# A hybrid decoder layer: other root, store and tile slots in its last product

## The chip, the core and the metric

The kernel runs on one core of a Trainium2 chip. The metric is the time of one execution on the device, in microseconds (us). TensorE is called PE, VectorE DVE, ScalarE ACT, GpSimd POOL and SyncE SP, as in the profile.

## What is computed

One decoder layer over 1024 tokens (plus 16 meta tokens) of width 1024, in float32. The part that matters here is the end of it:

```python
def rmsnorm(x, g):
    y = x * rsqrt(mean(x * x, axis=-1, keepdims=True) + EPS)     # EPS = 1e-6
    return y * g
...
    h = h + rmsnorm(mix, g_post_mix)
    u = rmsnorm(h, g_pre_ffn)
    f = square(relu(u @ w_ff1)) @ w_ff2      # w_ff1: 1024 x 4096, w_ff2: 4096 x 1024
    h = h + rmsnorm(f, g_post_ffn)
    return h[:, N_META:]
```

Before it come an input projection, sliding-window attention with sinks, a gated linear recurrence, and an output projection whose result is normed and added to the residual stream. The kernel writes that sum to `out` and later adds the normed result of the second feed-forward product to it.

## The kernel before

**Precision.** A float32 operand is split into a rounded part and a rest: `split` (L93 to L98) rounds on ACT (L95) and subtracts on DVE (L98). Each product is three matmuls, `mm3` (L121 to L125): high by high, high by low, low by high.

**The two feed-forward products.** Both are cut into 2 x 2 blocks and done with seven products of blocks instead of eight. For the second, `PLAN` (L1029 on) lists seven entries, i = 0 to 6: which blocks of the activations are added or subtracted, which blocks of `w_ff2` are, and into which parts of the result the product goes and with which sign. The sum runs over 512 rows of a block in eight steps, q = 0 to 7, so there are 56 steps n in order (i, q). In each, four token tiles j = 0 to 3 of 128 rows get six matmuls of 512 columns each. In i = 6 the last tile's 512 columns are done as two halves of 256 in two PSUM banks (`col_parts`).

**A step's operands.** `fetch_2(n)` (L1046) loads the one or two blocks of weights that the step needs, 512 KB each, on SP's queue. Where two blocks are added, some steps load the second with an accumulating DMA from POOL's queue into the first one's tile (L1055): for i < 6 those with q % 3 < 2, for i = 6 those whose second tag in `LASTW` is None. The others load both, and `prep_2(n)` (L1062) adds or subtracts them on DVE, splits the weights, combines and splits the activations. The loop fetches four steps ahead, from n = 45 on six.

**Slots.** All tiles in SBUF come from tagged pools (`bufs`, L55): "raw" has 2 slots, "e" 2, "ws" 4, "a" 16, "b" 17, "c" 8, "d" 4. A tile waits for a free slot of its tag. During the second product "a" holds the activation blocks fb["12"] and fb["21"] (eight each), the lower token tiles' sums facc["0", j], the broadcast gain and the finished tiles. "b" holds part of fb["11"], the upper tiles' sums facc["1", j], the combined and split activations, and four raw weight tiles of i = 6.

**Order.** A scheduler orders each engine's instructions by program order among those that are ready on its own clock of estimated durations, and gives out the slots as it goes. `behind` (L105) and `lut` (L81) add edges without a wait: an instruction comes behind a named one in its engine's order; `lut` chains all activations that use a table function (exponential, sigmoid, tanh, square root, GeLU) in program order.

**Norms of the result.** The result has eight token tiles: the upper four, facc["1", j], are complete after i = 5, the lower four, facc["0", j], only after i = 6.
- `rstd_of` (L155) turns partial means of squares into 1 / sqrt(sum + EPS): one add with EPS on DVE (L160; on POOL where there is one part), then a power of -0.5 on POOL (L164).
- `finish_early(j)` (L1120), for tiles 4 to 7, runs inside i = 5 and at the start of i = 6: two squares with their sums on ACT (L1117), `rstd_of`, one scaling on DVE (L1124), and an accumulating store to `out` from POOL's queue (L1128).
- `finish_half(j)` (L1132) runs in steps q = 1 to 4 of i = 6, for tiles 0 to 3: the square of the right half, which is complete by then (L1137). For tiles 2 and 3 it loads the rows of `out` into a "d" tile, adds EPS on POOL (L1144) and multiplies the right half by the gain on DVE (L1145).
- `finish_late(j)` (L1148) ends a tile. The last three steps (`LAST`) are done tile by tile, so that tile 0 ends first and tile 3 last. Tiles 0 and 1: add the product (L1154), square on ACT, `rstd_of`, one scaling (L1158) and an accumulating store from POOL (L1162). Tiles 2 and 3: add the product, squares and their sum on DVE (L1165), power on POOL (L1173), times the gain (L1175), then for each half scale and add the loaded rows (L1177) and a plain store, from SP and from ACT (L1180).

Of the kernel before, what the change touches and what calls it, by code (L numbers as in the profile page):

```python
# [9 lines left out]
F32 = mybir.dt.float32  # L10
F32R = mybir.dt.float32r
AF = mybir.ActivationFunctionType
ALU = mybir.AluOpType
# [3 lines left out]
P = 128  # L17
# [10 lines left out]
EPS = 1e-6  # L28
# [9 lines left out]
def hybrid_layer(  # L38
# [6 lines left out]
    nc = tc.nc  # L45
# [3 lines left out]
    const = ctx.enter_context(tc.tile_pool(name="const", bufs=1))  # L49
    small = ctx.enter_context(tc.tile_pool(name="small", bufs=4))  # L50
# [7 lines left out]
    def slot(tag, shape, dt=F32):  # L58
        uid[0] += 1
        return slab.tile(shape, dt, tag=tag, name=f"{tag}{uid[0]}", bufs=bufs[tag])  # L60
# [20 lines left out]
    def lut(*args, **kwargs):  # L81
        ins = nc.scalar.activation(*args, **kwargs).ins
        if last_lut[0] is not None:
            tc.add_manual_dep(
                ins, last_lut[0],
                mybir.DependencyInfo(
                    mybir.DependencyClass.NoSync, mybir.DependencyReason.DATA
                ),
                reason="lut",
            )  # L90
        last_lut[0] = ins.name
# [13 lines left out]
    def behind(name, *inss):  # L105
        for ins in inss:
            tc.add_manual_dep(
                ins, name,
                mybir.DependencyInfo(
                    mybir.DependencyClass.NoSync, mybir.DependencyReason.DATA  # L110
                ),
                reason="order",
            )
# [38 lines left out]
    half_pow = const.tile([P, 1], F32, name="half_pow")  # L152
    nc.gpsimd.memset(half_pow, -0.5)

    def rstd_of(ssq_parts, n=P):  # L155
        ms = small.tile([P, 1], F32, name="ms", tag="ms")
        if len(ssq_parts) == 1:
            nc.gpsimd.tensor_scalar(ms[:n], ssq_parts[0], EPS, None, op0=ALU.add)
        else:
            nc.vector.scalar_tensor_tensor(  # L160
                ms[:n], ssq_parts[0], EPS, ssq_parts[1], op0=ALU.add, op1=ALU.add
            )
        rs = small.tile([P, 1], F32, name="rs", tag="rs")
        nc.gpsimd.tensor_tensor(rs[:n], ms[:n], half_pow[:n], op=ALU.pow)  # L164
        return rs[:n]


# [249 lines left out]
    for b in range(2):  # L417
        pv = bank("pt", (P, 4, P))
        for i in range(4):
            o = NMETA + (4 * b + i) * P  # L420
# [366 lines left out]
    def combine(dst, x0, x1, op):  # L787
        return nc.vector.tensor_tensor(dst, x0, x1, op=op).ins  # L788
# [48 lines left out]
    def early(b, p0, hl):  # L837
        raw = slot("raw", [P, 2, 4, P])
        for k in range(2):
            w1_load(raw[:, k], b, p0 + k, 0, 1)  # L840
        split(*hl, raw)
        return {p0 + k: (hl[0][:, k], hl[1][:, k]) for k in range(2)}
# [49 lines left out]
    def p1(p, w):  # L892
        ya[p] = bank(("acc", "s")[p // 2 % 2])
        product(ya[p], w, b11, True)
        nc.scalar.copy(block("11", p), ya[p])
# [6 lines left out]
    for t in range(8):  # L902
# [12 lines left out]
        if t == 6:  # L915
            b21 = operand(u2f[0][2:4])
            hl = slot("b", ESH, F32R), slot("e", ESH, F32R)
            a11_early.update(early(0, 2, hl))

    for p in range(2):  # L920
        p1(p, a11_early[p])
    for p in range(2):
# [93 lines left out]
    def product_by_parts(acc, w, op):  # L1016
# [22 lines left out]


    LASTW = [
        ("raw", None), ("e", "raw"), ("b", None), ("b", None), ("raw", "e"), ("b", None),
        ("e", "raw"), ("b", None),
    ]

    def fetch_2(n):  # L1046
        i, q = steps[n]
        wx = PLAN[i][1]
        tags = (("raw", "e"), ("e", "raw"))[n % 2] if i < 6 else LASTW[q]
        raws = []  # L1050
        for (a, b), tag in zip(wx[:2], tags):
            if len(wx) == 3 and wx[2] is ADD and raws and (
                q % 3 < 2 if i < 6 else tag is None
            ):
                nc.gpsimd.dma_start(raws[0], w2v[q, a, b], accum_op=ADD)  # L1055
                break
            r = slot(tag, [P, 2, 512])
            nc.sync.dma_start(r, w2v[q, a, b])
            raws.append(r)
        return raws  # L1060
# [24 lines left out]
    w_low = [None]  # L1085
# [27 lines left out]
    COLS = (slice(0, 512), slice(512, 1024))  # L1113

    def squares(sq, src, n):
        p_ = small.tile([P, 1], F32, name=f"sq{n}", tag=f"sq{n}")
        nc.scalar.activation(sq, src, AF.Square, scale=RMS_SC, accum_out=p_)  # L1117
        return p_

    def finish_early(j):  # L1120
        acc = facc["1", j]
        o = slot("a", [P, D])
        ssq = [squares(o[:, c], acc[:, c], n) for n, c in enumerate(COLS)]
        nc.vector.scalar_tensor_tensor(  # L1124
            o, acc, rstd_of(ssq), gffn_b, op0=ALU.mult, op1=ALU.mult
        )
        t = 4 + j
        nc.gpsimd.dma_start(out[t * P : (t + 1) * P, :], o, accum_op=ALU.add)  # L1128
# [3 lines left out]
    def finish_half(j):  # L1132

        o = slot("a", [P, D])
        acc, c = facc["0", j], COLS[1]
        ssq = small.tile([P, 1], F32, name=f"late{j}", tag=f"late{j}", bufs=1)
        nc.scalar.activation(  # L1137
            o[:, c], acc[:, c], AF.Square, scale=RMS_SC, accum_out=ssq
        )
        h = None  # L1140
        if j > 1:
            h = slot("d", [P, D])
            nc.sync.dma_start(h, out[j * P : (j + 1) * P, :])
            nc.gpsimd.tensor_scalar(ssq, ssq, EPS, None, op0=ALU.add)  # L1144
            behind(w_low[0], combine(o[:, c], acc[:, c], gffn_b[:, c], ALU.mult))  # L1145
        halves[j] = h, o, ssq

    def finish_late(j, y, parts):  # L1148

        h, o, ssq = halves[j]  # L1150
        acc = facc["0", j]
        for k, c in enumerate(parts):
            yield k
            ins = combine(acc[:, c], y[k], acc[:, c], ALU.add)  # L1154
            if k == 1:
                behind(w_low[0], ins)
            if j < 2:
                w_low[0] = nc.vector.scalar_tensor_tensor(  # L1158
                    o, acc, rstd_of([squares(o[:, c], acc[:, c], 0), ssq]), gffn_b,
                    op0=ALU.mult, op1=ALU.mult,  # L1160
                ).ins.name
                nc.gpsimd.dma_start(out[j * P : (j + 1) * P, :], o, accum_op=ALU.add)  # L1162
                continue
            part = small.tile([P, 1], F32, name=f"part{k}", tag=f"part{k}")
            nc.vector.tensor_tensor_reduce(  # L1165
                out=o[:, c], in0=acc[:, c], in1=acc[:, c], scale=RMS_SC * RMS_SC,
                scalar=ssq, op0=ALU.mult, op1=ALU.add, accum_out=part,
            )
            ssq = part
        if j < 2:  # L1170
            return
        rs = small.tile([P, 1], F32, name="rs", tag="rs")
        nc.gpsimd.tensor_tensor(rs, ssq, half_pow, op=ALU.pow)  # L1173
        c = COLS[0]
        combine(o[:, c], acc[:, c], gffn_b[:, c], ALU.mult)  # L1175
        for c, eng in zip(COLS[::-1], (nc.sync, nc.scalar)):
            w_low[0] = nc.vector.scalar_tensor_tensor(  # L1177
                o[:, c], o[:, c], rs, h[:, c], op0=ALU.mult, op1=ALU.add
            ).ins.name
            eng.dma_start(out[j * P : (j + 1) * P, c], o[:, c])  # L1180
# [37 lines left out]
    for n, (i, q) in enumerate(steps):  # L1218
        while fetched < min(n + (4 if n < 45 else 6), len(steps)):
            raw_2[fetched] = fetch_2(fetched)  # L1220
            fetched += 1
        if n + 1 < len(steps):
            late = w_low[0]
            ready[n + 1] = prep_2(n + 1, "a" if n + 1 >= len(steps) - LAST else "ws")
        if q == 0:
            old = None if i == 0 else accs
            accs = [[bank(("acc", "s", "pt", "o")[j])] for j in range(4)]
            if i == 6:

                evict(5, 0, old[0][0], late)  # L1230
                accs[3] = [accs[3][0][:, :256], bank("acc")[:, :256]]
        if n < len(steps) - LAST:
            for j in range(4):
                for acc, cols in zip(accs[j], col_parts(i, j)):
                    step_mm(acc, j, q, ready[n], cols)
            del ready[n]
        if old and (q > 0 or i < 6) and q < 4:
            evict(i - 1, q, old[q][0], late)
        if i == 5 and q == 0:
            gffn_b = slot("a", [P, D])  # L1240
            nc.scalar.dma_start(gffn_b, g_post_ffn[0].partition_broadcast(P))
        if (i, q) in EARLY:
            finish_early(EARLY.index((i, q)))
        if i == 6 and 1 <= q < 5:
            finish_half(q - 1)
# [36 lines left out]
```

## Time and profile before

| | us |
|---|---|
| median of 3 runs | 974.02 (973.7 to 976.03) |
| the profiled execution | 972.95 |
| its span, from the first to the last instruction | 971.1 |
| PE busy in it | 953.7 |
| last product (i = 6), PE | about 918 to 964 |

The profile shows one execution. A row of an engine says when it starts, how long it takes, the engine, the line, the operation, the tiles written and read, the shapes, and in brackets how long the engine idled before and what released it. Starts are microseconds from the start of the span. Matmuls are pipelined, so one's row overlaps the next one's; the distance of their starts tells the rate. A DMA's row on an engine is its issue; the time to landing is told by the DMA view. The granted clock of PE was 0.999 in the mean.

### The profile page before, as it was taken

The page shows a single profiled execution, that of the slowest core. Times are in us where ns is not written, and L with a number is a line of the kernel's source. Part 1 is how long each engine was busy: PE and PEld are TensorE (multiplying, and loading weights), DVE is VectorE, ACT ScalarE, POOL GpSimd, SP SyncE. Part 2 cuts the span into 40 slices and gives each one's busy share as a digit, 9 for nine tenths or more (in the row PEclk, how much of TensorE's full clock was granted, in tenths as well). Part 3 has the DMA queues.
Part 4 walks back from the last instruction along what each step waited for, and adds up shares of the span by engine and source line. Part 5 has one row for each costly group of instructions (what it writes and reads, how often), then busy time and mean ns, then how long its engine had stood idle before and what let it go on. Part 6 is the DMA issues. An engine that isn't in the chain of part 4 may idle for free.

```text
span 971.1 us, 12490 instructions
## 1 busy us (share of the span) xinstructions
PE 953.7 (98%) x4782; PEld 803.0 (83%) x4782; DVE 674.6 (69%) x997; ACT 502.0 (52%) x809; POOL 82.4 (8%) x109
## 2 busy tenths in 40 slices
PE   6999999999999999999999999999999999999997
PEld 6999999888878887888888878888888888888786
DVE  6679997775976686665645465468557676779694
ACT  6646673567844554343555556555433344445350
POOL 4100000000002100000000000000111000003152
PEclk9999999999999999999999999999999999999999
DMA  9002001012234466576522264323678765548923
GB/s 296 23 1 66 23 23 44 23 48 64 84 119 144 159 207 209 173 251 209 198 87 87 97 206 125 114 87 114 172 176 198 186 224 187 184 163 195 223 80 87
DMA packets 88219, 130.13 MB, mean 134 GB/s; under 512 B 13624, under 2 KB 52552, under 8 KB 88160
## 3 DMA queue, kind: packets, MB, share of 16 engines
q1 hardware_dynamic: 79792, 107.33, 33.4%
q0 software_dynamic: 7792, 20.45, 10.1%
q10 hardware_dynamic: 576, 1.57, 0.4%
q8 instruction: 37, 0.61, 0.2%
q14 instruction: 22, 0.18, 0.1%
HBM read 110.46 MB, written 18.87 MB: 133 GB/s over the span
## 4 chain that ended last, share of the span: by engine, by line
PE 89%; DVE 4%; DMA 3%; issue 2%; ACT 1%; POOL 0%; SPq 0%; POOLq 0%; DVEq 0%; ACTq 0%
PE ps_acc L124 11%; PE ps_acc L123 11%; PE ps_acc L125 11%; PE ps_s L125 6%; PE ps_pt L123 6%; PE ps_s L124 6%; PE ps_pt L125 6%; PE ps_s L123 6%; PE ps_pt L124 6%; PE ps_o L124 5%; PE ps_o L123 5%; PE ps_o L125 5%; PE ps_o L506 2%; PE ps_pt L495 1%; DMA raw<-in_w_ff_dram 1%
## 5 line engine op out<-in xcount | busy, mean ns | idle before, releaser
L95 ACT CAST ws<-raw 128x1024 fp32r<-128x1024 f32 (+1 forms) x69 | 70.7, 1024 | 126.6 <-PE ps_o L124 48.8
L98 DVE TENSOR_TENSOR ws<-raw,ws 128x1024 fp32r<-128x1024 f32 (+1 forms) x70 | 83.5, 1194 | 59.6 <-ACT ws L95 59.5
L123 PE MATMUL ps_acc<-a,ws 128*128 128x256 f32 (+2 forms) x272 | 90.5, 333 | 0.6 <-DVE b L305 0.6
L124 PE MATMUL ps_acc<-a,ws 128*128 128x256 f32 (+2 forms) x272 | 89.8, 330 | 0.0
L125 PE MATMUL ps_acc<-a,ws 128*128 128x256 f32 (+2 forms) x272 | 89.4, 329 | 0.0
L98 DVE TENSOR_TENSOR b<-b,b 128x1024 fp32r<-128x1024 f32 (+2 forms) x48 | 57.6, 1201 | 24.7 <-PE ps_o L124 17.1
L95 ACT CAST ws<-e 128x1024 fp32r<-128x1024 f32 x43 | 45.0, 1046 | 55.3 <-PE ps_o L124 28.1
L95 ACT CAST b<-b 128x1024 fp32r<-128x1024 f32 (+2 forms) x48 | 49.4, 1030 | 42.8 <-DVE b L788 40.0
L98 DVE TENSOR_TENSOR ws<-e,ws 128x1024 fp32r<-128x1024 f32 x43 | 52.6, 1222 | 21.6 <-ACT ws L95 21.6
L123 PEld LDWEIGHTS ps_acc<-a,ws 128*128 128x128 f32 x272 | 51.2, 188 | 4.9 <-DVE b L305 0.8
L125 PEld LDWEIGHTS ps_acc<-a,ws 128*128 128x128 f32 x272 | 51.2, 188 | 4.6
L124 PEld LDWEIGHTS ps_acc<-a,ws 128*128 128x128 f32 x272 | 51.2, 188 | 3.9
L164 POOL TENSOR_TENSOR rs<-ms,half_pow 128x1 f32<-128x1 f32 (+1 forms) x31 | 21.3, 692 | 356.5 <-DVE ms L160 355.1
L123 PE MATMUL ps_acc<-ws,b 128*128 128x512 f32 (+1 forms) x120 | 46.3, 386 | 0.4 <-ACT ws L95 0.4
L124 PE MATMUL ps_acc<-ws,b 128*128 128x512 f32 (+1 forms) x120 | 46.5, 388 | 0.2 <-DVE ws L98 0.2
L125 PE MATMUL ps_acc<-ws,b 128*128 128x512 f32 (+1 forms) x120 | 46.2, 385 | 0.0
L123 PE MATMUL ps_pt<-ws,b 128*128 128x512 f32 x112 | 44.1, 394 | 0.0
L124 PE MATMUL ps_pt<-ws,b 128*128 128x512 f32 x112 | 44.1, 394 | 0.0
L125 PE MATMUL ps_pt<-ws,b 128*128 128x512 f32 x112 | 44.0, 393 | 0.0
L123 PE MATMUL ps_s<-ws,b 128*128 128x512 f32 x110 | 43.4, 395 | 0.0
L124 PE MATMUL ps_s<-ws,b 128*128 128x512 f32 x110 | 43.3, 393 | 0.0
L125 PE MATMUL ps_s<-ws,b 128*128 128x512 f32 x110 | 43.3, 393 | 0.0
(381 smaller groups left out, 2690.1 us busy)
## 6 DMA issues: line engine op xcount, KB each, us to landing
raw<-in_w_ff_dram SPq DMA_DIRECT2D x62, 512.0 KB, 4.0
e<-in_w_ff_dram SPq DMA_DIRECT2D x45, 512.0 KB, 3.6
d<-in_w_ff_dram SPq DMA_DIRECT2D x12, 512.0 KB, 3.8
s_dram<-d POOLq DMA_DIRECT2D x12, 512.0 KB, 3.9
raw<-in_w_in_dram SPq DMA_DIRECT2D x9, 512.0 KB, 3.6
c<-in_x_dram SPq DMA_DIRECT2D x8, 512.0 KB, 8.5
d<-in_x_dram SPq DMA_DIRECT2D x8, 512.0 KB, 4.6
out_dram<-raw SPq DMA_DIRECT2D x8, 512.0 KB, 2.6
```

Source lines behind the costliest of these rows:

```text
L95: nc.scalar.copy(hi, src)
L98: low = nc.vector.tensor_tensor(lo, src, f32(hi), op=ALU.subtract).ins
L123: nc.tensor.matmul(dst, lh, rh, start=start, stop=False, skip_group_check=True)
L124: nc.tensor.matmul(dst, lh, rl, start=False, stop=False, skip_group_check=True)
L125: nc.tensor.matmul(dst, ll, rh, start=False, stop=stop, skip_group_check=True)
L164: nc.gpsimd.tensor_tensor(rs[:n], ms[:n], half_pow[:n], op=ALU.pow)
L495: nc.tensor.transpose(pt[:, o : o + P], sn[h][:, 2 * bp + i, s * P : (s + 1) * P], ident,)
L506: nc.tensor.matmul(po[:, oc : oc + n], v, p_[:, pc : pc + n], start=first and k == 0, stop=last and k == 1, skip_group_check=True,)
```

## The change

1. A one-element square root, `load_root`, is put behind the output projection, ahead of the first feed-forward product.
2. `root_rstd` replaces `rstd_of` in `finish_early` and for the lower tiles: a square root on ACT, with one partial sum as the bias of the other, then a reciprocal on DVE. EPS is added to the first part by an Identity on ACT, in `finish_early` and in `finish_half`.
3. Tile 2 is finished as tiles 0 and 1 are, by an accumulating store from POOL; its rows of `out` are no longer loaded. Tile 3 keeps its plain stores; its left half is multiplied by the gain in two halves of 256 columns, each after its part of the sum.
4. For i = 2 to 5 the second raw tile of a step goes to an "a" slot, and the first alternates between "raw" and "e". In i = 6 the raw tile of q = 0 goes to a "b" slot.

```diff
+    eps_col = const.tile([P, 1], F32, name="eps_col")
+    nc.gpsimd.memset(eps_col, EPS)
+
+    def load_root():
+        root = small.tile([P, 1], F32, name="root", tag="root")
+        lut(root, eps_col, AF.Sqrt)
+
+    def root_rstd(ssq, bias, n=P):
+        sd = small.tile([P, 1], F32, name="sd", tag="sd")
+        lut(sd[:n], ssq, AF.Sqrt, bias=bias)
+        rs = small.tile([P, 1], F32, name="rs", tag="rs")
+        nc.vector.reciprocal(rs[:n], sd[:n])
         return rs[:n]
...
+    load_root()
     for p in range(2):
         p1(p, a11_early[p])
...
     LASTW = [
-        ("raw", None), ("e", "raw"), ("b", None), ("b", None), ("raw", "e"), ("b", None),
+        ("b", None), ("e", "raw"), ("b", None), ("b", None), ("raw", "e"), ("b", None),
         ("e", "raw"), ("b", None),
     ]
...
-        tags = (("raw", "e"), ("e", "raw"))[n % 2] if i < 6 else LASTW[q]
+        tags = LASTW[q]
+        if i < 6:
+            tags = ("raw", "e")[n % 2], "a" if i > 1 else ("e", "raw")[n % 2]
...
         ssq = [squares(o[:, c], acc[:, c], n) for n, c in enumerate(COLS)]
+        nc.scalar.activation(ssq[0], ssq[0], AF.Identity, bias=eps_col)
+        rs = root_rstd(ssq[1], ssq[0])
         nc.vector.scalar_tensor_tensor(
-            o, acc, rstd_of(ssq), gffn_b, op0=ALU.mult, op1=ALU.mult
+            o, acc, rs, gffn_b, op0=ALU.mult, op1=ALU.mult
         )
...
+        nc.scalar.activation(ssq, ssq, AF.Identity, bias=eps_col)
         h = None
-        if j > 1:
+        if j > 2:
             h = slot("d", [P, D])
             nc.sync.dma_start(h, out[j * P : (j + 1) * P, :])
-            nc.gpsimd.tensor_scalar(ssq, ssq, EPS, None, op0=ALU.add)
             behind(w_low[0], combine(o[:, c], acc[:, c], gffn_b[:, c], ALU.mult))
...
-            if j < 2:
+            if j < 3:
                 w_low[0] = nc.vector.scalar_tensor_tensor(
-                    o, acc, rstd_of([squares(o[:, c], acc[:, c], 0), ssq]), gffn_b,
+                    o, acc, root_rstd(squares(o[:, c], acc[:, c], 0), ssq), gffn_b,
                     op0=ALU.mult, op1=ALU.mult,
                 ).ins.name
...
             ssq = part
-        if j < 2:
+            if k == 1:
+                rs = root_rstd(ssq, 0.0)
+            w_low[0] = combine(o[:, c], acc[:, c], gffn_b[:, c], ALU.mult).name
+        if j < 3:
             return
-        rs = small.tile([P, 1], F32, name="rs", tag="rs")
-        nc.gpsimd.tensor_tensor(rs, ssq, half_pow, op=ALU.pow)
-        c = COLS[0]
-        combine(o[:, c], acc[:, c], gffn_b[:, c], ALU.mult)
```

More of the change, by code (lines that the diff above doesn't have):

```diff
@@ L164, in rstd_of @@
         nc.gpsimd.tensor_tensor(rs[:n], ms[:n], half_pow[:n], op=ALU.pow)
+        return rs[:n]
+    eps_col = const.tile([P, 1], F32, name="eps_col")
[8 more added lines that the diff above has]
+        nc.vector.reciprocal(rs[:n], sd[:n])
         return rs[:n]
```

## The prediction, made before the changed kernel was run

> **What bounds the kernel now.** I read the page first, then the waits of TensorE, then the rows of single engines around the one wait that the change can reach, and last the rows behind the last matmul.
>
> ```profile
> span 971.1 us, 12490 instructions
> PE 953.7 (98%) x4782; PEld 803.0 (83%) x4782; DVE 674.6 (69%) x997; ACT 502.0 (52%) x809; POOL 82.4 (8%) x109
> ```
>
> TensorE (PE) is the bound: busy 98% of the span, and PE makes up 89% of the chain of waits. So an edit counts only where PE waits or where PE has ended. In the rows of PE from 383 us to the end I looked for starts more than 0.26 us apart (neighbours of 512 columns start 0.23 apart). Up to 917 us there is one place, at 578 us, in code that the change doesn't touch. Then comes the first step of the last of the seven products of W2 (i = 6, q = 0):
>
> ```profile
> 917.25 0.40 PE L125 MATMUL ps_o<-ws,b 128*128 128x512 f32 x1
> 918.05 0.50 PE L123 MATMUL ps_acc<-ws,b 128*128 128x512 f32 x1 [0.40 <-ACT ws L95]
> ...
> 918.86 0.28 PE L123 MATMUL ps_o<-ws,b 128*128 128x256 f32 x1
> 919.31 0.50 PE L124 MATMUL ps_acc<-ws,b 128*128 128x512 f32 x1 [0.18 <-DVE ws L98]
> ```
>
> The starts say what this costs. 917.25 to 918.05 is 0.80 instead of 0.23: 0.57 lost. 918.86 to 919.31 is 0.45 instead of 0.23 (two halves of 256): 0.22 lost. The matmul after each of the two late ones comes 0.34 later instead of 0.23: 0.11 twice. Together **1.0 us**. ACT rounds these weights late because they land late; the chain of waits has it:
>
> ```profile
> 907.68 9.19 DMA raw<-in_w_ff_dram
> 916.96 1.05 ACT ws L95
> 918.03 1.24 DVE ws L98
> ```
>
> That transfer is the accumulating second load of q = 0 (L1055), and POOL issues it third:
>
> ```profile
> 892.44 1.21 POOL L1055 DMA_DIRECT2D b<-in_w_ff_dram  x1 [1.44 <-issue]
> ...
> 901.75 1.23 POOL L1055 DMA_DIRECT2D b<-in_w_ff_dram  x1 [7.11 <-PE ps_o L125]
> 902.51 1.41 POOL L1128 DMA_DIRECT2D out_dram<-a  x1
> 907.68 1.22 POOL L1055 DMA_DIRECT2D raw<-in_w_ff_dram  x1 [3.77 <-issue]
> 917.20 1.20 POOL L1055 DMA_DIRECT2D b<-in_w_ff_dram  x1 [8.29 <-issue]
> ```
>
> The DMA answer for these windows gives times to landing of 9.0, 5.6, 9.8, 9.2 and 5.3 us. 892.44 + 9.0 = 901.44, 901.75 + 5.6 = 907.35 and 907.68 + 9.2 = 916.88: each accumulating weight load starts 0.3 us after the one before has landed, whatever the blocks before POOL name. They go one at a time, and q = 0's is behind those of q = 2 and q = 3, which got their "b" slots (SyncE rows at 884.41 and 889.74) before q = 0 got its "raw" slot (892.98).
>
> PE's last matmul ends at 964.00 (963.72 + 0.28). What follows is 7.1 us of norm and store:
>
> ```profile
> 964.65 0.49 DVE L1165 CUSTOM_DVE_ANT_0 a<-a,part 128x256 f32<-128x256 f32 x1
> 965.06 0.08 DVE L1165 DVE_READ_ACCUMULATOR2_ANT part<- 128x1 f32 x1
> 965.18 0.69 DVE L788 TENSOR_TENSOR a<-a,a 128x512 f32<-128x512 f32 x1
> 965.29 0.99 POOL L1173 TENSOR_TENSOR rs<-part,half_pow 128x1 f32<-128x1 f32 x1 [2.87 <-DVE part L1165]
> 966.31 1.41 DVE L1177 SCALAR_TENSOR_TENSOR a<-a,rs,d 128x512 f32<-128x512 f32 x2 [0.44 <-POOL rs L1173]
> 967.09 0.36 SPq L1180 DMA_DIRECT2D out_dram<-a  x1
> 967.76 0.35 ACTq L1180 DMA_DIRECT2D out_dram<-a  x1
> ```
>
> So the change can reach 1.0 us at 917 and a part of the tail.
>
> **The change part by part.**
>
> 1. *Second raw tiles for i > 1 go to "a"* (fetch_2). This frees "raw" and "e" slots, so loads start earlier. PE has no wait from 580 to 917 us that it could end: **0**. "a" has 16 slots; the eight of fb["12"] fall free during i = 1, four are taken by facc["0"], four are left for four steps of look-ahead. If they ran short, a late pair would come back as a PE wait (rival E's kind).
>
> 2. *q = 0 of i = 6 takes "b" instead of "raw"* (LASTW). Its load comes first in program order among the "b" tiles, so it should take the slot of 884.41 and the POOL place of 892.44; by that row it lands at 901.4, 15 us before PE needs it, since rounding and subtracting take 1.05 + 1.23. **-1.0.** What is late next: q = 2 moves to the second place (907.4), ACT rounds it at 926.86; q = 3 to the third (916.9), q = 5 to 922.5, q = 7 to 928.7, and ACT rounds the last of these from 940 on. All have 9 us or more. One "b" slot more is held from 884 on: five tiles wait in 17 slots. DVE makes the first operand of i = 6 at 898.73, 18 us ahead of its use, so a slot less costs look-ahead and no time. Bounds: -1.0 (all of it) and 0 (the order on POOL stays).
>
> 3. *load_root.* One Sqrt of 128x1 and one table load on ACT. The row of table loads says 1.28 us, and at 255.43 the next ACTIVATE starts at 256.72, so a switch is 1.3. It has no operand to wait for and sits behind the last GeLU (259.87), so the scheduler can put it in ACT's first hole: 263.92 to 266.89, or 268.89 to 271.15, each longer than the 1.5 us that it needs. **0**; if it fell in front of the rounding at 271.15 that PE waits for, up to +1.5. The "ScalarE: Activation LUTs" page of the Trainium skill, "What ACT_TABLE_LOAD costs", adds a drain of 1.38 us and comes to 2.66 us a switch; the rows at 255.43 and 256.72 show none of that, and 2.66 would still fit the first hole.
>
> 4. *Roots on ACT for tiles 4 to 7 (finish_early).* Off: four adds on DVE (0.15) and four powers on POOL (0.56 to 1.57). On: an Identity and a Sqrt of 128x1 on ACT, a reciprocal on DVE. The 128x1 read of the accumulator takes 0.18 and the 128x128 ACTIVATE with a pointer scale 0.376; less 127 columns at 0.82 ns (0.63 at 512 columns, 1.05 at 1024) that is 0.27. I take 0.27 (bounds 0.18, 0.38). Reciprocal: 0.16, by 0.17 for 128x4 and 0.15 for the add. ACT +0.54 a tile, four times; ACT is 61% idle from 880 to 917, so PE hides it: **0**. Without this cover, 2.2.
>
> 5. *Tiles 0 to 2 (finish_half, finish_late).* For tile 2, finish_half loses one of two 512 KB loads on SyncE and a 0.61 us product on DVE; **0**, PE is running. Tile 2 in the tail: sum 959.79 to 960.48, Square and its read to 961.24 (0.76, as at 952.18), Sqrt to 961.54, reciprocal 961.58 to 961.74, scaling of 1024 columns (1.28) to 963.06, POOL's issue 0.69 later as for tile 1 (959.29 to 959.98): 963.75. Its store takes 5.1 us:
>
> ```profile
> out_dram<-a POOLq DMA_DIRECT2D x1, 512.0 KB, 5.1
> ```
>
>    so alone it lands at 968.85.
>
> 6. *Tile 3.* DVE is free at 962.97; then sum 0.37, squares 0.40, product 0.37: 964.1, so the last sum starts at 964.19 as before and the part is ready at 965.14. Then Sqrt (965.17 to 965.44) in place of POOL's 0.99, while DVE does the 256-column product (to 965.5), reciprocal to 965.66, scaling at 965.70 instead of 966.31: 0.61 sooner, so SyncE's store is issued at 966.48 and ACT's at 967.15. If DVE has the reciprocal ahead of the product, scaling starts at about 965.93: 0.38 sooner.
>
>    But now tile 2's accumulating store runs under the last two. The trace has this case one tile earlier: tile 1's accumulating store issued at 959.98, two 256 KB stores at 963.24 and 963.91, the last landed after 2.58, at 966.49, 6.51 behind the first issue; the DMA engines are busy from 961.0 to 965.9 without a break:
>
> ```profile
> DMA  0000000000000989993096899988900039910000
> ```
>
>    (40 slices of 0.55 us from 950 on). With nothing beside it a 256 KB store lands in 2.06, so before the last landing is at 967.76 + 2.06 = 969.82. After, 963.75 + 6.51 = 970.26: **+0.4**, although the arithmetic is 0.6 sooner. Bounds: -0.6 (the stores pass by) and +0.8 (the engines' work adds in full: 3.3 us for the store and 1.0 for each of the two behind the 0.4 to a landing).
>
> **Sum:** -1.0 + 0 + 0 + 0.4 = -0.6. The profiled execution took 972.95 (span 971.1 and 1.85 around it), so 972.35; the median of the runs is 1.07 above it. I put the change on the median: 974.02 - 0.6 = **973.4**.
>
> **The rivals.**
>
> A (forecast): the wait at 917 goes, the tail gives 0.4 back: 973.4. For it: the one-at-a-time rows of POOL. Chance 0.48.
>
> B: no gain at 917. The planner gives the first "b" slot to q = 2 again, or another first weight is late: the change doesn't do what it says. 974.02 + 0.4 = 974.4. Chance 0.16.
>
> C: the last stores aren't held up: -1.0 - 0.6, 972.4. For it: each packet of a small store is short. Against it: 2.5 and 2.6 us at 963 instead of 2.06. Chance 0.13.
>
> D: the DMA engines share out fully: +0.8, 973.8. The Trainium skill's "DMA: Bandwidth & Descriptors", "Queues, rings and completion order", says that an engine goes round its queues packet by packet; by that each short packet of the last stores would wait for one of the accumulating store's. The strip above agrees so far that nothing idles. Chance 0.09.
>
> E (slower): a slot is missing. Five waiting tiles hold "b" slots, and one operand for steps 45 to 48 is made a turn late. A slot turns over with a step, 24 matmuls of 0.23, so the wait is up to 5.5 us: 974.02 - 1.0 + 0.4 + 5.5 = 978.9 at the worst. It decides once the first operand of i = 6 is made later than some 914 instead of 898.73. Against it: 18 us of look-ahead. Chance 0.08.
>
> F (slower): Square and Sqrt are in different table sets. Then every finish switches twice, 2 x 1.28. PE hides all but tile 2's, between its sum and its root: 2.6 on DVE's queue ahead of tile 3, so 974.02 - 1.0 + 0.4 + 2.6 = 976.0. It decides from the first Sqrt behind a Square. The trace has Square running under the sets of Exp (first load, none before the first Exp) and of GeLU (after 255.43), none under Sqrt. The "Table sets" section of the same ScalarE page names relu, copy, identity and abs as in every set, and not Square. Chance 0.06.
>
> **How the numbers follow.** A measurement of this kernel tells about 0.3% from no change, 2.9 us: faster is below 971.1, slower above 976.9. A to D and F at its size lie inside; E lies above. Faster would need all of the 1.0 and twice what the tail can give: 0.03. Slower: E, and a part of F if a switch costs more: 0.12. Same: 0.85. The range takes A, B, C, D and F and the unknown costs: C's 972.4 less 0.4 for the scatter of the runs below their median, to F's 976.0: 972.0 to 976.0. E and what I haven't seen are left out.
>
> **What would show it.** Right: five L1055 rows into "b" after 885 us and none into "raw", PE's starts at 917 0.23 apart, eight ACT_TABLE_LOADs in all instead of seven, a 0.2 to 0.3 us Sqrt on ACT between DVE's last read of the accumulator and a reciprocal, and tile 2's store landing less than 1.5 us before the end of the last. Wrong: a PE wait of over 0.5 us anywhere from 580 on, more than eight table loads, or DVE behind PE by more than 1 us at tile 3.

## The result: 0.55% slower

The changed kernel takes 980.06 us (median of 7 runs, 977.81 to 982.02), the kernel before beside it 974.5 us. The ratio is 1.0055, 95% interval 1.0038 to 1.0072. The prediction said 973.4 us and 972.0 to 976.0. The time lies above that range, and the slower side had been given 0.12.

The profiled execution of the changed kernel took 979.69 us. Its page begins so:

```profile
span 977.9 us, 12493 instructions
PE 954.0 (98%) x4782; PEld 801.7 (82%) x4782; DVE 672.0 (69%) x995; ACT 507.9 (52%) x829; POOL 62.7 (6%) x101
```

PE does the same work in the same busy time (954.0 us, 953.7 before), at a granted clock of 0.998 in the mean, and POOL has lost a quarter of its work. The 6.8 us are waits of PE and a longer end. Setting the start of each matmul of one trace against the start of the same matmul in the other tells where they came. Shifts of under 0.3 us, which nearly cancel, are left out:

| place (us of the new trace) | later (+) or sooner (-) | step of the prediction that covers it |
|---|---|---|
| 266 to 272, output projection | +0.9 | 3, load_root: 0 |
| 466, first feed-forward product | +0.5 | none |
| 714, end of i = 1 | +1.9 | 1, new raw slots: 0 |
| 816 to 837, i = 3 | +4.3 | 1, new raw slots: 0 |
| 917 of before, start of i = 6 | -1.3 | 2, q = 0 in "b": -1.0 |
| behind the last matmul | +0.6 | 6, shared DMA: +0.4 |

### The profile page after: what moved, and what is told of

Its sections match the earlier page's. It is cut to its first block, busy times and chain, and to the rows that moved or that the text cites. A ratio compares the mean times of both kernels' runs of the same rounds, so it can differ in the third digit from the quotient of the medians.

```text
span 977.9 us, 12493 instructions
## 1 busy us (share of the span) xinstructions
PE 954.0 (98%) x4782; PEld 801.7 (82%) x4782; DVE 672.0 (69%) x995; ACT 507.9 (52%) x829; POOL 62.7 (6%) x101
## 5 line engine op out<-in xcount | busy, mean ns | idle before, releaser
L98 DVE TENSOR_TENSOR ws<-raw,ws 128x1024 fp32r<-128x1024 f32 (+1 forms) x69 | 82.2, 1192 | 37.4 <-ACT ws L95 37.3
L98 DVE TENSOR_TENSOR b<-b,b 128x1024 fp32r<-128x1024 f32 (+2 forms) x48 | 57.6, 1200 | 25.4 <-PE ps_o L124 17.2
L98 DVE TENSOR_TENSOR ws<-e,ws 128x1024 fp32r<-128x1024 f32 x43 | 52.5, 1222 | 14.7 <-ACT ws L95 14.7
L123 PE MATMUL ps_o<-ws,b 128*128 128x512 f32 (+1 forms) x108 | 41.5, 384 | 0.0
```

The lines of the kernel that those rows point to most:

```text
L98: low = nc.vector.tensor_tensor(lo, src, f32(hi), op=ALU.subtract).ins
L123: nc.tensor.matmul(dst, lh, rh, start=start, stop=False, skip_group_check=True)
```

## The profile after

**The new waits of PE.** The list of PE's waits between 700 and 930 us, first of the kernel before, then of the changed one (total, times, longest):

```profile
PE ps_acc L123 <- ACT ws L95: 0.4, 1, 0.4
PE ps_acc L124 <- DVE ws L98: 0.2, 1, 0.2
```

```profile
PE ps_acc L124 <- DVE ws L98: 4.9, 4, 1.7
```

The old wait at 917 is gone. In its place PE waits four times for a subtraction on DVE (L98): once at 714, three times in i = 3.

**i = 3.** DVE's rows of the changed kernel, then SP's load issues in the same stretch:

```profile
800.43 1.22 DVE L98 TENSOR_TENSOR ws<-e,ws 128x1024 fp32r<-128x1024 f32 x1
...
806.86 1.22 DVE L803 TENSOR_TENSOR e<-e,a 128x1024 f32<-128x1024 f32 x1 [3.48 <-issue]
808.01 1.22 DVE L98 TENSOR_TENSOR ws<-raw,ws 128x1024 fp32r<-128x1024 f32 x1
...
814.31 1.23 DVE L803 TENSOR_TENSOR raw<-raw,a 128x1024 f32<-128x1024 f32 x1 [3.95 <-issue]
815.45 1.22 DVE L98 TENSOR_TENSOR ws<-e,ws 128x1024 fp32r<-128x1024 f32 x1
...
821.20 1.23 DVE L803 TENSOR_TENSOR e<-e,a 128x1024 f32<-128x1024 f32 x1 [3.40 <-DMA e<-in_w_ff_dram]
822.34 1.22 DVE L98 TENSOR_TENSOR ws<-raw,ws 128x1024 fp32r<-128x1024 f32 x1
```

```profile
801.68 0.37 SPq L1076 DMA_DIRECT2D e<-in_w_ff_dram  x1
808.12 0.37 SPq L1076 DMA_DIRECT2D a<-in_w_ff_dram  x1
809.25 0.37 SPq L1076 DMA_DIRECT2D raw<-in_w_ff_dram  x1
815.56 0.37 SPq L1076 DMA_DIRECT2D a<-in_w_ff_dram  x1
816.70 0.37 SPq L1076 DMA_DIRECT2D e<-in_w_ff_dram  x1
```

Read the two together. L803 is the helper `combine`, which puts a step's two raw tiles together (in i = 3 the plan subtracts them; it is called the sum here, to tell it from the subtraction in `split`, L98). The subtraction at 800.43 reads the "e" tile of a step and frees it. SP's load into that slot is issued at 801.68. The trace has no landing for it, but the sum that needs it starts at 806.86, behind 3.48 us in which DVE does nothing. Only then comes the subtraction at 808.01. It needs nothing from that sum: its own "raw" tile was summed at 799.29 at the latest, and ACT had rounded it by 805.57. But it stands behind the sum in DVE's order. It in turn frees the slot for the load of 809.25, which the sum at 814.31 waits for, and so on. The step that is subtracted is k, the step that is summed is k + 3, since the first tiles now have four slots, two "raw" and two "e". One round of load (4.4 to 5.2), sum (1.14) and subtraction (1.14) is about 7 us (the subtractions from 808.01 on start 7.4 and 6.9 apart), while PE uses a step up in 24 x 0.23 = 5.5 us. DVE's lead over PE shrinks by some 1.5 us a step until PE waits:

```profile
823.62 0.51 PE L124 MATMUL ps_acc<-ws,b 128*128 128x512 f32 x1 [1.07 <-DVE ws L98]
830.63 0.50 PE L124 MATMUL ps_acc<-ws,b 128*128 128x512 f32 x1 [1.16 <-DVE ws L98]
837.45 0.50 PE L124 MATMUL ps_acc<-ws,b 128*128 128x512 f32 x1 [1.04 <-DVE ws L98]
```

The bracket shows less than the late start: the matmul before the first of these started at 822.16, and 822.16 to 823.62 is 1.46 instead of 0.23.

In the kernel before, a step takes both of its tiles from "raw" and "e", so the four slots hold fewer steps, and the order on DVE is the other way round. The subtraction of step k comes first, and the sum of k + 2 behind it:

```profile
801.97 1.23 DVE L98 TENSOR_TENSOR ws<-raw,ws 128x1024 fp32r<-128x1024 f32 x1 [1.50 <-ACT ws L95]
803.45 1.23 DVE L788 TENSOR_TENSOR raw<-raw,e 128x1024 f32<-128x1024 f32 x1 [0.25 <-DMA raw<-in_w_ff_dram]
```

So more slots gave a deeper look-ahead for the planner, and with it an order in which the deeper step's sum blocks the nearer step's subtraction.

**714 us.** SP's issues and the sum of i = 1's last pair of tiles in the changed kernel:

```profile
697.30 3.85 SPq L1076 DMA_DIRECT2D a<-in_w_ff_dram  x2
701.92 0.37 SPq L1076 DMA_DIRECT2D e<-in_w_ff_dram  x1
704.38 0.37 SPq L1076 DMA_DIRECT2D a<-in_w_ff_dram  x1
705.52 8.91 SPq L1076 DMA_DIRECT2D raw<-in_w_ff_dram  x2
```

```profile
712.81 1.22 DVE L803 TENSOR_TENSOR e<-e,raw 128x1024 f32<-128x1024 f32 x1 [6.11 <-DMA raw<-in_w_ff_dram]
```

In the kernel before, the same load and the same sum:

```profile
703.15 7.58 SPq L1058 DMA_DIRECT2D raw<-in_w_ff_dram  x2
```

```profile
709.11 1.22 DVE L788 TENSOR_TENSOR e<-e,raw 128x1024 f32<-128x1024 f32 x1 [4.86 <-DMA raw<-in_w_ff_dram]
```

Three loads into "a" for i = 2 and 3 (697.30, 700.78 in the first row's pair, 704.38) are issued as soon as the slots are free. The "raw" tile that DVE needs next is issued behind them at 705.52 and lands after 7.2 us; before it was issued at 703.15 and took 5.9. PE's work stood 1.75 us later by then than before, so of the 1.9 us some 0.6 is the later issue and 1.3 the longer transfer. Between 690 and 715 us the DMA engines move 225 GB/s, where they moved 164 before.

**The table load.** ACT behind the last GeLU:

```profile
259.78 1.14 ACT L82 ACTIVATE d<-d 128x512 f32<-128x512 f32 x2
260.92 1.28 ACT L82 ACT_TABLE_LOAD   x1
262.21 0.20 ACT L82 ACTIVATE root<-eps_col 128x1 f32<-128x1 f32 x1
262.32 1.03 ACT L95 CAST a<-d 128x1024 fp32r<-128x1024 f32 x1
```

The load did not go into the hole at 263.9. In the program the square root stands behind the whole output projection. But it waits for nothing, and the planner put it straight behind the GeLU, ahead of roundings that come earlier in the program. These follow 1.4 us later (the first at 262.32 instead of 260.90). PE's start behind 266.55 is 0.7 late. Behind 271.75 it waits 0.94 us from start to start, where it waited 0.80 before, so that only 0.14 is new there.

**The end.** PE's last matmul ends at 970.27, and 7.65 us follow (7.06 before). DVE and ACT, then the three stores:

```profile
970.59 0.42 DVE L803 TENSOR_TENSOR a<-ps_acc,a 128x256 f32<-128x256 f32 x1
971.04 0.48 DVE L1185 CUSTOM_DVE_ANT_0 a<-a,part 128x256 f32<-128x256 f32 x1
...
971.91 0.15 DVE L179 RECIPROCAL rs<-sd 128x1 f32<-128x1 f32 x1
972.10 1.41 DVE L1196 SCALAR_TENSOR_TENSOR a<-a,rs,d 128x512 f32<-128x512 f32 x2
```

```profile
970.36 0.86 POOL L1182 DMA_DIRECT2D out_dram<-a  x1 [3.60 <-issue]
```

```profile
972.88 0.36 SPq L1199 DMA_DIRECT2D out_dram<-a  x1
```

```profile
out_dram<-a ACTq DMA_DIRECT2D x1, 256.0 KB, 3.4
```

The scaling starts 1.83 us behind PE's end, 2.31 before: the root is 0.48 us faster. But ACT's store takes 3.4 us to land instead of 2.06, as tile 2's accumulating store (issued 970.36, landed 975.66) runs under it.

## The experiments

Theory T: the new raw slots in i = 2 to 5 cost about 6 us (1.9 + 4.3 in the profile), by DVE's order and by loads that come too early; the other parts cost and gain about 1 us each. Each set of kernels was timed against the kernel before on its own chip. The medians of that kernel were 971.95, 974.59, 973.6 and 974.77 us in the four sets, so ratios are compared, and only within one set where 0.1% matters.

**1. The raw slots of i < 6 as before, all else changed.**

```diff
-        tags = LASTW[q]
-        if i < 6:
-            tags = ("raw", "e")[n % 2], "a" if i > 1 else ("e", "raw")[n % 2]
+        tags = (("raw", "e"), ("e", "raw"))[n % 2] if i < 6 else LASTW[q]
```

> The changed kernel with the slots of the raw tiles for i < 6 as before; q = 0 of i = 6 stays in b, the roots and tile 2 stay as changed. Theory T (the new slots put the sums of two weight blocks ahead of older subtractions in DVE's order, and each then waits for a load that such a subtraction has to release): PE's waits at 714 and 816 to 837 us go, 1.9 + 4.3 us; left are +0.9 for the table load at 261, -1.3 for the wait at 917 and +0.6 in the tail, so the kernel before +0.2: about 974.7. Rival R2 (the roots on ACT and the longer tail cost the time): stays near 980.

972.76 us, ratio 1.0007 (0.9998 to 1.0017). No wait of PE is left between 700 and 930 us: the list that held 4.9 us is empty. The 917 wait stays away. So the slots are the loss, and without them the rest of the change is worth nothing measurable: -1.3 at 917 is paid back by +0.9 at 266 and +0.4 at the end (7.47 us).

**2. The new raw slots alone, in the kernel before.**

```diff
-        tags = (("raw", "e"), ("e", "raw"))[n % 2] if i < 6 else LASTW[q]
+        tags = LASTW[q]
+        if i < 6:
+            tags = ("raw", "e")[n % 2], "a" if i > 1 else ("e", "raw")[n % 2]
```

> The kernel before with only the new slots of the raw tiles for i = 2 to 5. Theory T: +6.2 on the kernel before (1.9 at the end of i = 1, 4.3 in i = 3), about 980.7, with PE waits of 1.2 to 2 us for DVE's subtraction of the weights, and the wait at 917 as before. R2: within 1 us of the kernel before.

977.18 us, ratio 1.0043 (1.0028 to 1.0058). PE's waits in the same window:

```profile
PE ps_acc L124 <- DVE ws L98: 2.9, 5, 1.0
PE ps_acc L123 <- ACT ws L95: 0.6, 1, 0.6
```

The slots alone make most of the loss, at the same places (711 and 818 to 831 us); by the ratio it is 4.2 us, where 6.2 was expected. The second line is the old wait at 917, which these slots do not touch.

**3. q = 0 of i = 6 in "b" alone, in the kernel before.**

```diff
-        ("raw", None), ("e", "raw"), ("b", None), ("b", None), ("raw", "e"), ("b", None),
+        ("b", None), ("e", "raw"), ("b", None), ("b", None), ("raw", "e"), ("b", None),
```

> The kernel before with only the raw tile of q = 0 of i = 6 in a b slot. If this alone ends the wait at 917, PE's starts there are 0.23 apart and the time is 1.0 to 1.3 below the kernel before, about 973.2. Rival: the wait went because POOL lost its powers or because PE came 7.5 us later; then the wait stays and the time is that of the kernel before.

A miss: 977.58 us, ratio 1.0051 (1.0036 to 1.0066), where 1 us less was expected. The wait at 917 is gone as expected, but PE waits 5.1 us at 901.6. POOL's rows, then DVE's:

```profile
893.07 1.21 POOL L1055 DMA_DIRECT2D b<-in_w_ff_dram  x1 [2.01 <-issue]
902.41 1.22 POOL L1055 DMA_DIRECT2D b<-in_w_ff_dram  x1 [8.13 <-issue]
903.17 1.05 POOL L164 TENSOR_TENSOR rs<-ms,half_pow 128x1 f32<-128x1 f32 x1
```

```profile
904.26 1.28 DVE L1124 SCALAR_TENSOR_TENSOR a<-b,rs,a 128x1024 f32<-128x1024 f32 x1 [8.90 <-POOL rs L164]
905.46 1.22 DVE L98 TENSOR_TENSOR ws<-e,ws 128x1024 fp32r<-128x1024 f32 x1
```

POOL's second accumulating load waits 8.13 us until the first has landed (at 902.1). The power of an early tile's norm is queued behind it. DVE's scaling waits 8.90 us for that power, and the subtraction that PE needs stands behind the scaling. In the changed kernel there is no power on POOL, so the same load order blocks nobody. The two edits belong together: moving the roots to ACT is what lets this one pay.

**4. The changed kernel with its sums held behind the subtraction of two steps earlier, i = 2 to 5.** Slots and loads stay as in the change.

```diff
             if i == 6:
                 behind(w_low[0], ins)
+            elif i > 1:
+                behind(rests[n - 2], ins)
...
-        w_low[0] = split(wh, wl, raws[0]).name
+        w_low[0] = rests[n] = split(wh, wl, raws[0]).name
...
```

> The changed kernel whole, but for i = 2 to 5 the sum of a step's two weight blocks is put behind the subtraction of step n - 2 in DVE's order, as it stood before the change; slots and loads stay. Theory T: the four waits of PE in i = 3 go, -4.3 on the changed kernel, about 975.8; the 1.9 at the end of i = 1 stays, since the sum that waits there is of i = 1 and isn't moved. Rival R1 (too few a slots, or the loads ahead of time take the DMA engines' time): the loads are as late as they are and the time stays near 980.

972.79 us, ratio 1.0003 (0.9993 to 1.0013). All waits of i = 3 are gone; one is left, at 713:

```profile
PE ps_acc L124 <- DVE ws L98: 2.2, 1, 2.2
```

So in i = 3 the order on DVE was the cause, not the number of slots and not the traffic. The wait at 713 weighs less than this profile suggests: it shows the slowest of the ten executions (975.54 us), and the median is that of kernel 1 in the same set (972.76), which has no such wait. So what the wait costs in most executions isn't shown. The order is now that of the kernel before, with the subtraction first:

```profile
806.18 1.22 DVE L98 TENSOR_TENSOR ws<-raw,ws 128x1024 fp32r<-128x1024 f32 x1 [1.50 <-ACT ws L95]
807.32 1.22 DVE L803 TENSOR_TENSOR raw<-raw,a 128x1024 f32<-128x1024 f32 x1
```

**5. Kernel 1, and the table load later.** The one-element root now reads the sum of squares of the first tile behind the output projection, so it can't start before that.

```diff
-    load_root()
...
+        if t == 0:
+            load_root(ssq2)
```

> e1 with the lone square root fed by the sum of squares of the first output tile, so that its table load falls behind ACT's square at 285 us, where ACT idles for 1.8 us and PE has work. Theory: the 0.9 us by which PE starts the output projection later in e1 (266.7 and 272.0) goes, the kernel before -0.2, about 0.9 us below e1. Rival: the 0.9 us is not the table load's; then as e1, the kernel before +0.7.

972.61 us, ratio 0.9975 (0.9962 to 0.9988). The table load now starts at 286.0, and PE's late starts between 235 and 280 us fall from 1.62 to 0.66, what the kernel before has (0.67). So the trace shows that the 0.9 us came from the place of the table load. What that is in medians isn't told, as kernel 1 was timed in another set.

**6. Kernel 1, and tile 2 with plain stores**, roots on ACT throughout.

```diff
-        if j > 2:
+        if j > 1:
...
-            if j < 3:
+            if j < 2:
...
-            if k == 1:
+            if k == len(parts) - 1:
                 rs = root_rstd(ssq, 0.0)
...
-        if j < 3:
+        if j < 2:
             return
```

> e1 with tile 2 finished as before the change (rows of out loaded, plain stores from SP and ACT), its root and tile 3's on ACT. Theory (tile 2's accumulating store takes the DMA engines from the last two stores): from PE's last matmul to the end 6.4 us instead of 7.5 in e1 and 7.06 before; 1.1 us below e1, the kernel before -0.4. Rival: the tail is longer through DVE's order at tile 3; then 7.5 stays.

973.68 us, ratio 0.9983 (0.9969 to 0.9997). The end shrinks to 6.77 us, from 7.47 in kernel 1 and 7.06 in the kernel before; 6.4 was expected. Tile 2's accumulating store costs 0.7, and the roots on ACT alone gain 0.3.

**7. The roots on ACT and the accumulating store alone**: the change without new raw slots in any step and without q = 0 in "b".

```diff
-        ("b", None), ("e", "raw"), ("b", None), ("b", None), ("raw", "e"), ("b", None),
+        ("raw", None), ("e", "raw"), ("b", None), ("b", None), ("raw", "e"), ("b", None),
```

(on top of kernel 1)

> The changed kernel with all slots of raw tiles as before, i = 6's q = 0 too: roots on ACT and tile 2's accumulating store are left. Theory: table load +0.9, tail +0.5, the wait at 917 stays as in the kernel before, so the kernel before +1.4. Rival: POOL without its powers ends the wait at 917 by itself; then +0.4.

975.45 us, ratio 1.0005 (0.9994 to 1.0017). The wait at 917 is still there (late starts of 1.35 in all), so freeing POOL of the powers doesn't end it. It takes the slot of kernel 3 and the roots together.

**8. Kernels 5 and 6 together.**

> e5 and e6 together: roots on ACT, first tile of i = 6 in b, the later table load, tile 2 with plain stores. Theory: the two gains add, -0.9 and -1.1 on e1: the kernel before -1.3, about 0.13% faster. If the gains of single steps are lost again elsewhere, within 0.5 us of the kernel before.

972.13 us, ratio 0.9972 (0.9959 to 0.9985). The same kernel once more, beside the next two:

> The same kernel as the best version before, run beside the two others: ratio 0.997 (0.9958 to 0.9985), no start of TensorE more than 0.5 us late between 700 and 960 us, 6.8 us from TensorE's last matmul to the end. If the wait of 0.5 to 0.9 us at 466 us shows in one execution and not in another of the same kernel, it belongs to the execution; if it shows in both or in neither, to the kernel.

971.95 us, ratio 0.9980 (0.9971 to 0.9989). This is faster than the kernel before by 0.2 to 0.3%, 1.9 and 2.7 us. The traces account for 1.6 of it (1.3 at 917 and 0.3 at the end); where the rest comes from isn't shown. The two profiles of it also bear on the 0.5 us at 466: late starts between 440 and 600 us sum to 0.67 in one and 2.7 in the other, so the size of that wait differs from one execution to the next. Whether the change plays a part stays open: a start over 0.25 us late at 466 to 468 us shows in nine of the eleven profiles with roots on ACT, and in none of the three without (the kernel before, kernels 2 and 3). Kernels 6 and 7 have one more start 0.7 us late, at 759, which no run here explains.

**9. Kernel 4 with "a" slots only from i = 3 on**, to take away early loads at 700.

```diff
-            tags = ("raw", "e")[n % 2], "a" if i > 1 else ("e", "raw")[n % 2]
+            tags = ("raw", "e")[n % 2], "a" if i > 2 else ("e", "raw")[n % 2]
```

> The kernel after with its sums held behind the subtraction two steps earlier (as in the pinned run), and "a" slots for the second raw tiles only from i = 3 on, so that no load into "a" is issued at 697 to 704 us, while i = 1 runs. Theory T (the wait of 2.1 to 2.6 us at 713 comes from those early loads crowding the DMA engines): the load of the second tile of i = 1's last step is issued near 703 again and lands before its need; the wait at 713 is below 0.6 us; the loads into "a" of i = 3 on cost nothing. Then 1.5 to 2.5 us less than the pinned run had against the kernel before: ratio 0.998 to 0.999. Rival (another operation is late at the end of i = 1, for example the accumulating load on POOL or the sum's place in DVE's order): the wait at 713 stays at 2 us or more, ratio 1.000 to 1.001.

A miss in the sum: 980.25 us, ratio 1.0067 (1.0047 to 1.0088). Of what was expected, one part held. The wait at 713 is gone: the "raw" tile's load is issued at 705.70 behind two "a" loads instead of three, and lands after 4.3 us instead of 7.2, though it is issued no earlier than in the changed kernel (705.52). (The expectation that no "a" load would be issued there was wrong; i = 3's first two take the free slots.) But two new waits came, at 757 and 777, of ACT's rounding:

```profile
758.90 1.04 ACT L95 CAST ws<-e 128x1024 fp32r<-128x1024 f32 x1 [8.45 <-DMA e<-in_w_ff_dram]
...
779.08 1.04 ACT L95 CAST ws<-raw 128x1024 fp32r<-128x1024 f32 x1 [9.21 <-DMA raw<-in_w_ff_dram]
```

POOL's accumulating loads of i = 2, first of this kernel, then of kernel 1, where PE has no such wait:

```profile
745.77 1.20 POOL L1073 DMA_DIRECT2D raw<-in_w_ff_dram  x1 [7.89 <-DVE b L803]
753.03 1.22 POOL L1073 DMA_DIRECT2D e<-in_w_ff_dram  x1 [6.06 <-issue]
```

```profile
744.64 1.20 POOL L1071 DMA_DIRECT2D e<-in_w_ff_dram  x1 [11.27 <-DVE b L803]
752.08 1.22 POOL L1071 DMA_DIRECT2D raw<-in_w_ff_dram  x1 [6.24 <-issue]
```

They have changed places. The sum of step 18 (i = 2, q = 2) was held behind the subtraction of step 16, so that subtraction freed its "raw" slot first, step 20's load went out ahead of step 19's, and so did its accumulating half. They go one at a time, so step 19's "e" tile landed at 758.8 instead of 751.8. The wait at 777 follows from the next held sum: step 21's stands at 761.72, behind the late subtraction of 759.98, and keeps the "raw" slot of step 22 until 762.96 (755.60 in kernel 1).

**10. Kernel 8 with the slots and the held sums of kernel 9.**

> The version with the best time so far (tags as before, table load late, tile 2 with plain stores) plus the second raw tiles in "a" slots from i = 3 on with the sums held in their old order. Theory: TensorE has no wait between 720 and 917 us that an earlier load could end, so the slots bring nothing: equal to that version within 0.1%, ratio 0.997 to 0.998. Rival (more slots hide waits that the trace shows only as scattered starts): 1 us faster or more, ratio below 0.9965. Second rival (the loads into "a" still crowd others at the start of i = 3): a new wait of over 0.5 us between 740 and 900 us, ratio 0.998 or more.

977.71 us, ratio 1.0036 (1.0023 to 1.0049), with the same two waits (2.22 and 2.93 us from start to start): the second rival's sign, and the same swap of POOL's loads (745.83 "raw", 751.84 "e"). The next kernel tests that cause.

**11. Kernel 10 with the sums held only from i = 3 on.** i = 2 has its old slots and its old order.

```diff
-            elif i > 1:
+            elif i > 2:
                 behind(rests[n - 2], ins)
```

> The best version before, plus "a" slots for the second raw tiles from i = 3 on, with the sums held behind the subtraction two steps earlier from i = 3 on only, so that i = 2 keeps both its old slots and its old order. Theory (slots and order of a step belong together; the waits at 757 and 777 in the two runs before came from holding i = 2's sum, whose second tile sits in one of the four "raw" and "e" slots, behind a subtraction that waits for a load): no wait over 0.6 us of TensorE from 700 to 960 us, and no gain either, as nothing there waits in the version without the slots: ratio 0.997 to 0.998, sum of late starts between 700 and 900 us below 1 us. Rival (the two loads into "a" that are still issued at 697 crowd others, in any order): a wait of 2 us or more between 713 and 780 us, ratio 1.000 or more.

971.4 us, ratio 0.9972 (0.9960 to 0.9983). No start of PE is over 0.5 us late between 600 us and the end, and POOL's loads are in their old order (744.12 "e", 750.56 "raw"). The two "a" loads are still issued at 697.9 and 701.4 and harm nobody. So the new slots with the right order cost nothing, and they bring nothing either: the ratio is that of kernel 8.

## Why the prediction was wrong, point by point

- **Step 1, the raw slots: forecast 0, measured +6.2 in the profile (1.9 + 4.3), 4.2 us by the ratio of kernel 2.** This is the step that failed. It argued that PE has no wait from 580 to 917 us that earlier loads could end, and so priced only the gain. The edit also has two costs that it left out. The slots change the order that the planner writes for DVE, and an instruction that waits for a load holds up all behind it (kernel 4: the order alone is the 4.3). And loads that come early take their share of the DMA engines from a load that is due (kernel 9: without the third "a" load the wait at 713 is gone). That the third load alone is to blame was shown with the sums held in order, not in the change's own order, and in single profiles: in the medians kernel 4 loses nothing measurable against kernel 1 (972.79 and 972.76), so there the order takes back the whole loss. The prediction's sign, a PE wait of over 0.5 us from 580 on, was the right thing to look for.
- **Step 2, q = 0 in "b": -1.0, measured -1.3.** Right, for the reason given. But kernel 3 shows a condition that the step didn't name: it pays only because step 4 takes the powers off POOL. Alone it costs 5 us.
- **Step 3, load_root: 0, measured +0.9.** The bounds (0 to 1.5) held and the value was wrong. The step had noted that the instruction waits for nothing and concluded that it could go into a hole; the planner put it ahead of the roundings instead, at the first place that the chain of table functions left open, and not where it is written.
- **Step 4, roots of tiles 4 to 7: 0.** Right: in kernel 1 PE doesn't wait there.
- **Steps 5 and 6, the end: +0.4, measured +0.59** (0.41 in kernel 1). Right in mechanism. The arithmetic was 0.48 sooner, not 0.61, and tile 2's store was issued 0.09 behind PE's end, not 0.25 ahead of it. Sqrt of 128x1 took 0.29 with its bias from a tile (0.27 forecast) and 0.20 with the constant bias of tile 3. Kernel 6 shows both halves: 0.7 lost to the shared store, 0.3 gained by the root.
- **The rivals.** B, C and D were about steps that went nearly as forecast. F fell: there are eight table loads, one more than before, so Square, Identity and the roundings run under the set that Sqrt loaded. On the switch itself, the rows at 260.92 and 262.21 are 1.29 apart; the drain of 1.38 us that the Trainium skill adds ("ScalarE: Activation LUTs", "What ACT_TABLE_LOAD costs") doesn't show here either. E named the right kind of loss (an operand made a turn late), but put it on the "b" slots at i = 6, where nothing happened, and gave it 0.08.

## To carry to other kernels

More buffers are not free when a planner or an in-order engine sits behind them. Before pricing a new slot at zero, follow one slot round its loop (who frees it, which load that starts, who waits for the load, what is queued behind that waiter) and ask whether anything behind the waiter is what frees the next slot; if so the steps run one after the other, here 7.0 us against 5.5. An operation with nothing to wait for may be put far ahead of the place where it is written, here in front of work that a busier engine needs; give it an operand that becomes ready where its engine is idle, as kernel 5 does. And an edit that reorders a queue (here POOL's loads) is judged with all that the queue carries: the same line gained 1.3 us with the powers gone and lost 5 us with them there.

## What the runs showed of the hardware

**A short wait of PE can cost nearly twice its length.** In kernel 4 PE started no matmul from 712.68 to 715.33. The table of stretches (us, busy times, then PE's granted clock, DMA share, GB/s) shows full clock before and 0.61 after:

```profile
700.00:712.00 12.00, 12.00 (x54) 9.80 (x54) 3.71 (x4) 4.13 (x5) 1.23 (x1) 1.00 0.90 237
715.30:719.50 4.20, 4.17 (x12) 3.31 (x13) 3.50 (x3) 1.97 (x2) 1.20 (x1) 0.61 0.98 298
720.00:730.00 10.00, 10.00 (x45) 8.07 (x43) 6.26 (x6) 3.48 (x4) 1.90 (x2) 1.00 0.84 194
```

The matmuls of 512 columns start 0.427 apart there instead of 0.23, and the wait of 2.4 us costs 4.1. The same happened behind 5.1 us in kernel 3 (0.54 from 906.8 to 910.4), 2.22 us in kernel 10 (0.57 from 759 to 763) and 3.2 us in kernel 9 (0.50 from 780 to 785). It did not behind 2.06 us at 714 in the changed kernel, nor behind 2.26 us at 757 in kernel 9 (all from start to start of two matmuls). So the length alone doesn't decide: 2.22 us was followed by the drop, 2.26 us was not. The Trainium skill ("TensorE: Matmul & The Clock Gate", Part 1) has the clock halved after an idle window of about 3.4 us that runs free of the kernel's start. The halved rate agrees with the runs. But drops also followed gaps of 2.22 and 2.64 us, which are shorter than that window. The matmuls stay 0.427 apart for some 3.5 us in kernels 3, 4 and 10, and for nearly 6 in kernel 9.

**Accumulating loads from POOL go one at a time** wherever two met in the traces here: the next is issued about 0.3 us after the one before has landed (745.77 and its landing at 752.72, then 753.03 in kernel 9), and what is queued on POOL behind it waits too (the power in kernel 3). What holds them back isn't shown. One of 512 KB took 5.3 us at best (695.96 in the kernel before) and up to 10.1 us beside other loads (893.64 in the second profile of kernel 8).
